# Two-layer decoder trunk on one core: order of the score matmuls, the affine steps, a weight-row sum and the last head's output-weight rows

## The chip, the core and the metric

The kernel runs on one core of a Trainium2 chip. A core has five engines that run in parallel, each with its own instruction queue, served in order: TensorE (PE, matmuls; its weight loads are listed as PEld), VectorE (DVE), ScalarE (ACT), GpSimd (POOL) and SyncE (SP, which only issues transfers). Transfers between the chip's memory and the core's SRAM go through 16 DMA engines; SP, ACT and POOL issue them into queues of their own. Matmuls write into eight PSUM banks of 128 partitions by 512 float32.

The metric is the device time of one execution in microseconds (us). The clock granted to TensorE was 0.997 of full speed in the profiled execution.

## The reference

A decoder trunk of two layers over 512 positions of width 1024 in float32, batch 1. Layer 0 mixes tokens with a causal pooling over windows, layer 1 with causal differential attention; a SwiGLU FFN of inner width 2816 follows each. Four layer norms in all.

```python
def _diff_attention(x, w_qkv, w_o, lam_p, subln_g, rel_table, lambda_init):
    qkv = x @ w_qkv
    # 8 heads, each with two score maps of width 64 and one value of width 128
    lam = exp(sum(lp[0]*lp[1])) - exp(sum(lp[2]*lp[3])) + lambda_init
    for qb in range(S // 128):
        s = einsum('bhcqd,bhckd->bhcqk', q_block, k[..., :kend]) * 64**-0.5
        s = where(rel >= 0, s + bias, -inf)
        p = softmax(s)
        a = p[:, :, 0] - lam * p[:, :, 1]
        outs.append(einsum('bhqk,bhkv->bhqv', a, v[:, :, :kend]))
    o = concatenate(outs)
    o = o * rsqrt(mean(o**2) + eps) * subln_g * (1 - lambda_init)
    return o @ w_o

def _swiglu(x, w_gate, w_up, w_down):
    return (silu(x @ w_gate) * (x @ w_up)) @ w_down

for i in range(2):
    h = pool(x) if i == 0 else diff_attention(x)
    x = layernorm(ALPHA * x + h)
    x = layernorm(ALPHA * x + swiglu(x))
```

## The kernel before, in words

**Numbers.** Every float32 matmul is made of three products of reduced-precision (float32r) operands: a value is split into a high part (a cast on ScalarE, line 123) and a low part (a subtraction on VectorE, line 124), and high x high, low x high, high x low are added in PSUM (`mm3`, lines 148 to 151). `split` does this; `ready(n)` (from line 126) splits weight rows up to number n, and `fetch` (line 107) loads the raw rows five ahead of that on SP's queue. Two of the raw rows, 74 and 75 of the weight array, are the sum of two rows each: a plain load on SP and then an accumulating transfer on POOL (line 113).

**Seven products in place of eight.** Most of the large matmuls are cut in 2x2 blocks and computed as seven products of sums of blocks, named P1, Q5, P6, Q3, P7, P2, Q4 in the order in which they run (`DOWN`). The second half of an FFN (the loop around line 936) runs these seven over six pairs of rows: 42 items, `d_0` to `d_41`; P2 is items 30 to 35, Q4 items 36 to 41. `prepare(j + 5, j + 4)` stands ahead of item j's matmuls (`multiply`, line 928): it issues the transfers and the splits of items some places ahead. Row sums are held in `r` (loads on SP, lines 541 and 544) and split into `d_..h` and `d_..l`; the left side is split into `xs`. Q4's last three items are done one half at a time, with the layer norm's pieces between (its reciprocal root is on POOL, line 199).

**The weight-row sums of the attention's values.** The values of all heads are computed in the same way: `values(p, ...)` (line 1076) for P1, P2, P6, P7, Q4, Q5, Q3, two weight pairs each. P6 uses `vt0`, `vt1`, the split of `tall`; P7 uses `vs0`, `vs1`, the split of `short` (part of the tile `vals`); Q4 uses `vu0`, `vu1`, the split of `tall` with one more row pair added. `tall` is the sum of three row pairs of 1 MB each: a load on SP and two accumulating transfers on POOL, all issued by `tall_step`, which the loop calls at the start of each product and which acts at Q3, P2 and Q4. The third accumulate into `tall` (line 1296) is issued after `vt0` and `vt1` have been split. `short` is a load on SP (line 1016) and an accumulate on POOL (line 1017). The tile of `tall` shares its buffer with the gains and offsets of the layer norms (`load_gb`), one buffer for both.

**The attention's heads.** The loop over heads (around line 1333) runs, in one pass h: the last part of head h-1's combination; the split of head h-1's values (`vh`, `vl`); in passes 1 to 4 one `affine` (lines 225 to 228), which multiplies and adds the previous norm's gain and offset on one 128-row block of the residual, two VectorE operations; queries and keys of head h and their splits, with `ready` between for rows that are needed later; head h-1's transposes (line 1183); scores of head h for the four blocks of 128 query rows (line 1142), softmax (VectorE line 1153, ScalarE line 1158), head h-1's product with the values (`mix`); and combinations of the two maps (VectorE lines 1167 to 1172). A pair of score banks is filled by three rounds of two matmuls, one on each half of the 128 rows of the array, one for each map. `root` and `scaled` are the norm of a head's output: `root(h-2)` and `scaled(h-2)` (tile `rso`) run two passes later.

In the last pass, h = 7, `ready` also splits rows of the output weight: `w92` and `w93` ahead of the query, `w94` and `w95` ahead of `scaled(5)` and of the split of the key. After the loop the output matmuls run (`wo`), one 128-row block s at a time, on rows `w92` to `w95`, with the norm of head 6, the transposes and the product of head 7 between them.

**What sets the order.** Each engine works its queue in the order in which the program names its instructions; waits between engines are put in by the framework from the tiles that are read and written. PSUM banks are handed out in turn, eight in all.

Of the kernel before, what the change touches and what calls it, by code (L numbers as in the profile page):

```python
# [16 lines left out]
ALU = mybir.AluOpType  # L17
# [7 lines left out]
SB = S // P  # L25
# [29 lines left out]
def trunk(ctx, tc, x, wall, pscale, lam_p, subln, table, lng, lnb, band, first, onehot, out):  # L55
    nc = tc.nc
# [145 lines left out]
    def norm(n, s, done=None):  # L202
        if (n, s) not in scales:
            spread_of(n, s)
        mv, rs = scales.pop((n, s))
        z = res[:, s, :]
        if not done:
            nc.vector.tensor_scalar(
                z, z, scalar1=mv[:, 0:1], scalar2=rs, op0=ALU.subtract, op1=ALU.mult
            )  # L210
            return
        gb = gbs[n]
        halves = [slice(d * 512, (d + 1) * 512) for d in range(2)]
        for c in halves:
            nc.vector.scalar_tensor_tensor(
                z[:, c], z[:, c], mv[:, 0:1], gb[:, 0, c], op0=ALU.subtract, op1=ALU.mult
            )
        for c in halves:
            nc.vector.scalar_tensor_tensor(
                z[:, c], z[:, c], rs, gb[:, 1, c], op0=ALU.mult, op1=ALU.add  # L220
            )
            done(s, c)

    def affine(n, s):
        z = res[:, s, :]
        gb = gbs[n]
        nc.vector.tensor_tensor(z, z, gb[:, 0, :], op=ALU.mult)
        nc.vector.tensor_tensor(z, z, gb[:, 1, :], op=ALU.add)
# [36 lines left out]
    def two_rows(c):  # L265
        return wall[vrow[c] : vrow[c] + 2].rearrange("r p t -> p r t")

    talls = []

    def tall_step(p):  # L270
        if p == "Q3":
            talls.append(keep.tile([P, 2, D], F32, tag="gb", name="tall"))
            nc.sync.dma_start(out=talls[0], in_=two_rows(0))
        elif p in ("P2", "Q4"):
            nc.gpsimd.dma_start(
                out=talls[0], in_=two_rows(1 if p == "P2" else 2), accum_op=ALU.add
            )

    lines = dram.tile([HEADS, LINE], F32, name="lines")

# [223 lines left out]
    def ffn(layer, late):  # L504
        n = 2 * layer + 1
        final = n == 2 * DEPTH - 1
# [3 lines left out]
        with tc.tile_pool(name=f"ffn{layer}", bufs=1) as fp:  # L510
# [58 lines left out]
            for k in range(HALF):  # L569
                j0 = index[k] = len(chunks)  # L570
                c = c0 + 4 * k
# [16 lines left out]
            for kind, j in steps:  # L588
                c, pair = chunks[j]
# [347 lines left out]
            done = store if final else None  # L937
            for p in DOWN:
                j0 = DOWN.index(p) * len(PAIRS)
                if not final:  # L940
                    tall_step(p)
                if p in ("P1", "Q5", "P2"):
                    banks[p] = [bank(f"{p}_{layer}_{s}") for s in range(2)]
                accs = banks[{"P1": "P1", "Q5": "Q5", "Q3": "Q5", "P2": "P2"}.get(p, "P1")]
                together = len(PAIRS) - (tail if p == "Q4" else 0)
                for i in range(together):
                    j = j0 + i
                    prepare(j + 5, j + 4)
                    if p == "Q4":
                        if i == together - 1:  # L950
                            prepare(len(items), len(items))
                            ready(c1 + FB + 2)
                        for s in range(2):
                            if i == s:
                                spread_of(n, s)
                            if i == s + 1:
                                norm(n, s)
                    multiply(j, accs, range(2))
                for s in range(2):
                    if p == "P1":  # L960
                        add_to(s, 0, accs[s], ALPHA)
                    elif p == "Q5":
                        add_to(2 + s, 1, accs[s], ALPHA)
                    elif p == "P6":
                        add_to(s, 1, accs[s], ALPHA, op=ALU.subtract)
                    elif p == "Q3":
                        add_to(s, 1, accs[s])
                        stat(n, s, 1)
                    elif p == "P7":
                        add_to(2 + s, 1, accs[s], op=ALU.subtract)  # L970
                        stat(n, 2 + s, 1)
                    elif p == "P2":
                        add_to(s, 0, accs[s])
                        stat(n, s, 0)
                    elif p == "Q4":
                        if s == 0 and not final:
                            turn(n, 0)
                        for i in range(len(PAIRS) - tail, len(PAIRS)):
                            if final and s == 0:
                                prepare(j0 + i + 5, j0 + i + 5)  # L980
                                if i == 1:
                                    spread_of(n, 0)
                                    spread_of(n, 1)
                                if i == 2:
                                    norm(n, 0, done)
                            multiply(j0 + i, accs, (s,))
                        add_to(2 + s, 0, accs[s], ALPHA)
                        stat(n, 2 + s, 0)
                        spread_of(n, 2 + s)
                        if final and s == 0:  # L990
                            norm(n, 1, done)
                        norm(n, 2 + s, done)
                        if not final:
                            if s == 0:
                                turn(n, 1)
                            ready(c1 + FB + 3 + s)
            base[0] = c1 + FB


    def attention():  # L1000
        n = 2
        with tc.tile_pool(name="attn", bufs=1) as ap:
            lp = ap.tile([P, 4, HD], F32, tag="bias", name="lp", bufs=2)
            nc.sync.dma_start(
                out=lp.rearrange("p a b -> p (a b)"),
# [52 lines left out]
            where = [base[0]]  # L1058
# [75 lines left out]
            def scores(h, q):  # L1134
                (qh, ql), (kh, kl) = qk[h, "q"], qk[h, "k"]
                wide = max((q + 1) * P, 256)
                accs = [bank(f"s{h}_{q}_{c}") for c in range(2)]
                qs = slice(q * P, (q + 1) * P)
                for i, (a, b) in enumerate(((qh, kh), (ql, kh), (qh, kl))):
                    for c in range(2):  # L1140
                        r = slice(c * HD, (c + 1) * HD)
                        nc.tensor.matmul(  # L1142
                            accs[c][:, :wide], a[r, qs], b[r, :wide], start=i == 0, stop=i == 2
                        )
                maps[h, q] = accs
# [186 lines left out]
            last = HEADS - 1  # L1332
            for h in range(HEADS):
                if h > 0:
                    combine(h - 1, 3)
                if h > 0:
                    split_values(h - 1)
                if h == 0:
                    scalars()
                if 0 < h <= SB:  # L1340
                    affine(n - 1, h - 1)
                if h == SB + 1:
                    load_gb(n)
                if h + 1 < HEADS:
                    load_bias(h + 1)
                if h > 0:
                    accs = [bank(f"{nm}{h}") for nm in "qk"]
                    w = take(2)
                    ready(where[0] + {1: 3, last: 2}.get(h, 1))
                    query(accs[0], w[0])  # L1350
                    split_query(h, "q", accs[0])
                    if h > 1:
                        root(h - 2)
                    query(accs[1], w[1])
                    ready(where[0] + (4 if h in (1, last) else 2))
                    if h > 1:
                        scaled(h - 2)
                    split_query(h, "k", accs[1])
                    if h == 1:
                        w = take(2)  # L1360
                        for r in range(2):
                            values("Q3", r, vc, w[r])
                        for s in range(2):
                            combined(part(0, 1, s), vc[s], part(0, 1, s), ALU.subtract)
                    transposed(h - 1)
                start_scores(h)
                for q in range(2):
                    scores(h, q)
                    softmax(h, q)
                if h == 0:  # L1370
                    for s in range(2):
                        combined(part(1, 1, s), vc[s], part(1, 1, s), ALU.subtract)
                for q in (2, 3):
                    scores(h, q)
                if h > 0:
                    mix(h - 1)
                for q in (2, 3):
                    combine(h, q - 2)
                    softmax(h, q)
                combine(h, 2)  # L1380
# [144 lines left out]
```

## Time and profile before

| | |
|---|---|
| median of 3 runs | 948.29 us (948.05 to 949.07) |
| the profiled execution's own time | 948.47 us |
| its span in the profile | 946.7 us |
| TensorE's granted clock | 0.997 |
| TensorE busy | 931.2 us, 5712 matmuls |
| VectorE, ScalarE, GpSimd busy | 787.3, 513.8, 126.5 us |
| moved by DMA | 211 MB, mean 223 GB/s |

The profile lists instructions as: start (us), duration (us), engine, line, operation, output <- inputs, partitions x elements, count; in square brackets how long the engine stood before it and what released it. A matmul's listed duration overlaps the next one's start, since matmuls are pipelined; consecutive starts show the rate. A DMA's row on its issuing engine is only the issue; landing times stand in the views by tile and by queue. In the view of waits, a row is engine, line, what it waited for, total us, times, longest. In the chain of waits a row is start, length and what held the last-ending work up.

### The profile page before, as it was taken

To read this page: it belongs to the slowest core of one execution; us is meant where nothing else is said; L and a number is where in the kernel's file an instruction comes from. 1 tells how busy PE (TensorE), PEld (TensorE's weight loads), DVE (VectorE), ACT (ScalarE), POOL (GpSimd) and SP (SyncE) were. 2 spreads that over 40 slices of the span, in tenths; PEclk is the share of its full clock that TensorE was granted. 3 is DMA by queue.
4 is the path that set the end of the run, shared out by engine and by line. 5 is a ranking of instruction groups with operands and counts; after the bars stand their busy time and mean duration, and the time that the engine had idled before them with its cause. 6 is when DMAs were issued, how large, how long until landed. Compare 5 with 4: busy or idle time off the path is not lost.

```text
span 946.7 us, 14942 instructions
## 1 busy us (share of the span) xinstructions
PE 931.2 (98%) x5712; PEld 829.9 (88%) x5712; DVE 787.3 (83%) x1158; ACT 513.8 (54%) x819; POOL 126.5 (13%) x152
## 2 busy tenths in 40 slices
PE   9999999999999999999999999999999999999996
PEld 8898899999988878887888878998899999988884
DVE  8858989999988489968887886789779999987778
ACT  6752344555564357666878753843345554664450
POOL 4120211110001201101111100211111110001101
PEclk9999999999999999999999999999999999999998
DMA  8386988986868996875666522396988886878952
GB/s 240 125 267 225 327 265 273 269 251 215 256 209 270 350 314 189 211 196 150 155 160 138 141 90 81 118 325 214 270 252 248 251 278 202 258 248 276 349 169 90
DMA packets 86038, 211.11 MB, mean 223 GB/s; under 512 B 15140, under 2 KB 26660, under 8 KB 85966
## 3 DMA queue, kind: packets, MB, share of 16 engines
q1 hardware_dynamic: 43420, 117.16, 37.5%
q0 software_dynamic: 18768, 58.20, 24.8%
q10 hardware_dynamic: 23778, 34.78, 10.2%
q8 instruction: 45, 0.74, 0.3%
q14 instruction: 27, 0.22, 0.1%
HBM read 173.40 MB, written 36.72 MB: 222 GB/s over the span
## 4 chain that ended last, share of the span: by engine, by line
PE 82%; DVE 9%; ACT 3%; DMA 3%; issue 2%; POOL 0%; DVEq 0%; ACTq 0%; POOLq 0%
PE A L861 17%; PE P L928 9%; PE C L861 9%; PE B L861 4%; PE Q L928 3%; PE g L151 3%; PE u L149 3%; PE u L150 3%; PE u L151 3%; PE g L149 3%; PE g L150 3%; PE va L1076 2%; PE s L1142 2%; DMA r<-tsum 1%; DMA r<-in_wall 1%
## 5 line engine op out<-in xcount | busy, mean ns | idle before, releaser
L607 DVE TENSOR_TENSOR raw<-raw,raw 128x1024 f32<-128x1024 f32 x56 | 68.3, 1219 | 0.5
L123 ACT CAST xs<-hid 128x512 fp32r<-128x512 f32 (+1 forms) x60 | 34.7, 582 | 24.4 <-DVE hid L775 24.4
L124 DVE TENSOR_TENSOR xs<-hid,xs 128x512 fp32r<-128x512 f32 (+1 forms) x60 | 38.5, 643 | 7.8 <-ACT xs L123 7.8
L1158 ACT ACTIVATE p<-p,mn 128x128 f32<-128x128 f32 (+3 forms) x64 | 35.2, 552 | 12.4 <-DVE mn L1153 12.4
L249 ACT ACTIVATE y<-pt,bT,gT 128x128 f32<-128x128 f32 x80 | 30.1, 456 | 19.4 <-PE pt L235 19.4
L706 POOL DMA_DIRECT2D b<-in_wall x20 | 14.0, 706 | 170.8 <-DMA tsum<-b 70.4
L767 POOL DMA_DIRECT2D xs<-ssum x24 | 17.4, 726 | 141.6 <-PE Q L928 68.5
L199 POOL TENSOR_TENSOR rs<-rs,mhalf 128x1 f32<-128x1 f32 x16 | 12.5, 784 | 152.0 <-DVE rs L198 112.6
L639 DVE TENSOR_TENSOR hid<-sg,u 128x512 f32<-128x512 f32 x16 | 11.0, 687 | 26.1 <-PE u L151 14.1
L743 ACT CAST v<-u 128x512 fp32r<-128x512 f32 x22 | 13.6, 620 | 27.7 <-DVE u L741 27.7
L706 POOL DMA_DIRECT2D hid<-in_wall x24 | 18.7, 823 | 74.4 <-DMA tsum<-hid 43.9
L1153 DVE CUSTOM_DVE_ANT_0 p<-s,bias 128x128 f32<-128x128 f32 (+3 forms) x64 | 28.0, 485 | 0.7 <-PE s L1142 0.7
L124 DVE TENSOR_TENSOR xt<-y,xt 128x512 fp32r<-128x512 f32 x20 | 13.6, 690 | 12.1 <-ACT xt L123 12.1
L190 DVE BATCH_NORM_STATS2 st<-res 128x6 f32<-128x512 f32 x32 | 22.2, 695 | 1.1
L887 ACT ACTIVATE sg<-sg 128x512 f32<-128x512 f32 x14 | 8.9, 633 | 25.7 <-DVE sg L880 25.7
L707 POOL DMA_DIRECT2D hid<-in_wall x12 | 14.8, 1233 | 58.5 <-DMA hid<-in_wall 51.1
L655 ACT CAST xs<-hid 128x1024 fp32r<-128x1024 f32 x8 | 8.4, 1051 | 26.0 <-DVE hid L672 11.6
L1142 PE MATMUL s<-heads 64*128 64x256 f32 (+2 forms) x168 | 20.0, 353 | 1.1 <-ACT heads L123 0.8
L1142 PEld LDWEIGHTS s<-heads 64*128 64x128 f32 x168 | 14.1, 185 | 5.2 <-issue 1.0
L1172 DVE SCALAR_TENSOR_TENSOR p<-p,sm,p 128x128 f32<-128x128 f32 (+3 forms) x32 | 17.7, 552 | 1.1
L876 DVE TENSOR_TENSOR hid<-C,hid 128x512 f32<-128x512 f32 x14 | 9.7, 691 | 10.4 <-PE C L861 8.8
L872 ACT COPY hid<-C 128x512 f32<-128x512 f32 x14 | 8.2, 589 | 18.5 <-PE C L861 18.5
(1187 smaller groups left out, 3666.3 us busy)
## 6 DMA issues: line engine op xcount, KB each, us to landing
raw<-in_wall SPq DMA_DIRECT2D x122, 512.0 KB, 4.8
r<-tsum SPq DMA_DIRECT2D x40, 512.0 KB, 4.5
hid<-in_wall POOLq DMA_DIRECT2D x36, 512.0 KB, 7.4
b<-in_wall POOLq DMA_DIRECT2D x30, 512.0 KB, 6.0
r<-in_wall SPq DMA_DIRECT2D x30, 512.0 KB, 4.6
tsum<-hid ACTq DMA_DIRECT2D x24, 512.0 KB, 5.6
ssum<-v ACTq DMA_DIRECT2D x22, 512.0 KB, 4.3
tsum<-b ACTq DMA_DIRECT2D x20, 512.0 KB, 4.9
```

Of the source, the lines that this page charges most:

```text
L123: nc.scalar.copy(dst_h, src)
L124: (low or nc.vector).tensor_tensor(dst_l, src, dst_h.bitcast(F32), op=ALU.subtract)
L149: nc.tensor.matmul(acc, ah, bh, start=start, stop=False)
L150: nc.tensor.matmul(acc, ah, bl, start=False, stop=False)
L151: nc.tensor.matmul(acc, al, bh, start=False, stop=stop)
L249: nc.scalar.activation(y[:, k, :], pt[:, k * P : (k + 1) * P], AF.Identity, bias=bT[:, n, kk : kk + 1], scale=gT[:, n, kk : kk + 1],)
L607: tt(t, raws[pair[0]], raws[pair[1]], op=ALU.add)
L706: nc.gpsimd.dma_start(out=t[:, j], in_=src[:, j])
L861: nc.tensor.matmul(o, w[:, c], x[:, kk, :], start=p in ("P1", "Q5", "P2") and f + kk + e == 0, stop=p in ("Q4", "Q3", "P2") and (f, kk, e) ...
L928: nc.tensor.matmul(accs[s], x[:, k, r], y[:, c], start=first and k == 0 and e == 0, stop=last and k == m - 1 and e == 2, skip_group_check= ...
L1142: nc.tensor.matmul(accs[c][:, :wide], a[r, qs], b[r, :wide], start=i == 0, stop=i == 2)
L1158: nc.scalar.activation(p, p, AF.Exp, bias=mn[:, q, c : c + 1], scale=-1.0, accum_out=sm[:, q, c : c + 1],)
```

## The change

Four things move; no matmul is added or removed.

- In `scores`, each round queues the second map's matmul ahead of the first map's.
- `tall_step` is called by step number: the load of `tall` at the start of P2 (it was Q3's start), the first accumulate at the third item of Q4 (it was P2's start), the second after the whole loop (it was Q4's start), so behind the `ready` calls of Q4's end that issue the accumulates of rows 74 and 75. The attention's set-up follows directly, with the load and the accumulate of `short`.
- The `affine` steps run in passes 2 to 5 in place of 1 to 4, and the next gains and offsets are loaded in pass 6 in place of 5.
- In pass 7 `ready` takes three output rows (`w92` to `w94`) ahead of the query, none ahead of the split of the key, and `w95` after head 6's product with the values, ahead of the first combination of head 7.

```diff
-    def tall_step(p):
-        if p == "Q3":
+    def tall_step(step):
+        if step == 0:
             talls.append(keep.tile([P, 2, D], F32, tag="gb", name="tall"))
             nc.sync.dma_start(out=talls[0], in_=two_rows(0))
-        elif p in ("P2", "Q4"):
-            nc.gpsimd.dma_start(
-                out=talls[0], in_=two_rows(1 if p == "P2" else 2), accum_op=ALU.add
-            )
+        else:
+            nc.gpsimd.dma_start(out=talls[0], in_=two_rows(step), accum_op=ALU.add)
...
             for p in DOWN:
                 j0 = DOWN.index(p) * len(PAIRS)
-                if not final:
-                    tall_step(p)
+                if p == "P2" and not final:
+                    tall_step(0)
...
+                    if (p, i) == ("Q4", 2) and not final:
+                        tall_step(1)
                     multiply(j, accs, range(2))
...
                             ready(c1 + FB + 3 + s)
+            if not final:
+                tall_step(2)
             base[0] = c1 + FB
...
                 for i, (a, b) in enumerate(((qh, kh), (ql, kh), (qh, kl))):
-                    for c in range(2):
+                    for c in (1, 0):
...
-                if 0 < h <= SB:
-                    affine(n - 1, h - 1)
-                if h == SB + 1:
+                if 1 < h <= SB + 1:
+                    affine(n - 1, h - 2)
+                if h == SB + 2:
                     load_gb(n)
...
-                    ready(where[0] + {1: 3, last: 2}.get(h, 1))
+                    ready(where[0] + {1: 3, last: 3}.get(h, 1))
...
-                    ready(where[0] + (4 if h in (1, last) else 2))
+                    ready(where[0] + {1: 4, last: 3}.get(h, 2))
...
                 if h > 0:
                     mix(h - 1)
+                if h == last:
+                    ready(where[0] + 4)
                 for q in (2, 3):
                     combine(h, q - 2)
                     softmax(h, q)
```

## The prediction

> **What bounds the kernel now.** I read the page first, then TensorE's waits, then the chain of waits, then timelines around each wait that the change touches. The page's first section:
>
> ```profile
> PE 931.2 (98%) x5712; PEld 829.9 (88%) x5712; DVE 787.3 (83%) x1158; ACT 513.8 (54%) x819; POOL 126.5 (13%) x152
> ```
>
> TensorE is busy 98% of the span. No matmul is removed, so the time moves only where the matmul stream stands still. The view of TensorE's waits lists those places (engine, line, releaser: total us, times, longest):
>
> ```profile
> PE P L928 <- DVE xs L124: 0.6, 1, 0.6
> ...
> PE vc L1076 <- DVE w78l L124: 0.5, 1, 0.5
> ```
>
> Each is one stall. A wait counts from the modelled end of the previous matmul, so what a stall costs is better read from start to start, against the 0.23 us at which 512-wide matmuls follow each other undisturbed. Everything else (VectorE 83%, DMA) matters only through when it lets TensorE go on. The sum is made against the profiled execution, 948.47 us (span 946.7 and 1.8 around it); the median of the runs is 948.29, so 0.18 is taken off at the end. About 0.2% (1.9 us) is what this measurement can tell from no change.
>
> **Weight-row sums, the gain.** Row loads of the first FFN's last phases come late while the sums' three 1 MB transfers run. The chain of waits, and TensorE's timeline there:
>
> ```profile
> 328.93 11.06 DMA r<-in_wall
> ```
> ```profile
> 341.29 0.39 PE L928 MATMUL P<-d_29h,xs 128*128 128x512 f32 x1
> 341.71 0.50 PE L928 MATMUL P<-d_30h,xs 128*128 128x512 f32 x1
> 342.04 0.40 PE L928 MATMUL P<-d_30l,xs 128*128 128x512 f32 x1
> 343.05 0.73 PE L928 MATMUL P<-d_30h,xs 128*128 128x512 f32 x2 [0.61 <-DVE xs L124]
> ```
>
> The gaps are 0.42 and 1.01 between starts where 0.23 is usual: 0.19 + 0.78 = 0.97 us. (A smaller one, 0.33, 0.10 too long, is left out.) A row transfer took 11.06 us, in a stretch in which both accumulating transfers of `tall` are in flight:
>
> ```profile
> L275 POOL DMA_DIRECT2D tall<-in_wall x2: 1208/1218/1227, 324.4 to 337.7; - x2
> ```
>
> After the change none of the three is issued before P2. I take the whole 0.97 as won; bounds 0 (the row loads fill the DMA by themselves) and -0.97, as the stall cannot give more than itself.
>
> **Weight-row sums, the loss.** What is moved must still land in time. The second accumulate was issued at 337.7, and its first reader, ScalarE's cast `vt0h`, ran at 394.23: 56 us of cover. Now GpSimd issues it after the loop, behind the accumulate into the second added row (raw75). GpSimd's timeline and the landings, by tile (minimum, median, maximum) and by issue (KB, us to landing):
>
> ```profile
> 381.95 0.90 POOL L113 DMA_DIRECT2D raw<-in_wall  x1 [2.25 <-ACT xt L123]
> ...
> 386.69 1.21 POOL L1017 DMA_DIRECT2D vals<-in_wall  x1 [3.63 <-DMA vals<-in_wall]
> ```
> ```profile
> DMA to landing us min/median/max: 4.0/7.1/9.9
> ```
> ```profile
> vals<-in_wall POOLq DMA_DIRECT2D x1, 1024.0 KB, 10.9
> tall<-in_wall POOLq DMA_DIRECT2D x1, 1024.0 KB, 8.5
> ```
>
> raw75's accumulate lands at 381.95 + 9.9 = 391.85 (the maximum is its own, as the longest of this queue's row loads there). The next 1 MB accumulate of the same queue, into `vals`, was issued at 386.69 and landed at 386.69 + 10.9 = 397.59. So it came 5.74 us behind raw75, although issued 5.2 us ahead of raw75's landing: I read this as a queue served in order. The moved accumulate is issued at 382.85, ahead of `vals`, and takes that place: it lands at 391.85 + 5.74 = 397.6, `vals` at 403.3. Now the readers, ScalarE, VectorE and TensorE in turn:
>
> ```profile
> 394.23 1.06 ACT L123 CAST vt0h<-tall 128x1024 fp32r<-128x1024 f32 x1
> ...
> 397.60 1.05 ACT L123 CAST vs0h<-vals 128x1024 fp32r<-128x1024 f32 x1 [0.87 <-DMA vals<-in_wall]
> ```
> ```profile
> 397.59 1.28 DVE L1259 TENSOR_TENSOR vals<-va,vals 128x512 f32<-128x512 f32 x2
> ```
> ```profile
> 398.42 0.47 PE L1076 MATMUL va<-vt0h,heads 128*128 128x512 f32 x1
> ...
> 409.43 0.39 PE L1076 MATMUL va<-vu0h,xt 128*128 128x512 f32 x1
> ```
>
> `vt0h` starts at 397.6 instead of 394.23, 3.37 late. Behind it VectorE does `vt0l`, `vt1l`, then reads both `va` banks (397.59), which product P6 overwrites; the first of the two reads ended at 397.59 + 0.64 = 398.23, and P6 began at 398.42: 0.19 of slack. So P6 starts 3.37 - 0.19 = 3.2 us late. ScalarE's `vt1h` and the query's square wait behind `vt0h`, but scores need those much later. `vals` at 403.3 instead of 397.6 delays `vs0h` by 5.7 against 3.2 that TensorE is late already; `vs0` is used 5.6 us after P6's start (24 matmuls of 0.23), at 407.2, and its cast and subtract (1.05 + 1.22) end at 405.6: covered. The third accumulate (issued when `vt1l` is read, about 401.2) lands 8.5 later at 409.7; `vu0`'s cast and subtract end at 412.0, and TensorE comes to it at 409.43 + 3.2 = 412.6: just covered. Bounds: 0, if the moved accumulate lands by 394.4; and with 8.5 us behind raw75 (the `tall` row) in place of 5.74, +5.9. I take +3.2, as the `vals` row is the same size, queue and moment.
>
> One rule of the Trainium skill speaks the other way: the page "DMA: Bandwidth & Descriptors", section "Bandwidth", has 6.15 us for 1 MB issued from GpSimd. Counted from issue that would land the transfer at about 389, before anybody reads it, and the sum would lose the 3.2. The trace has 8.5 and 10.9 for such transfers when they accumulate, so I let the rows decide.
>
> **Affine steps.** Head 1, the second of the two affine operations and what follows it on VectorE, and TensorE:
>
> ```profile
> 431.98 1.22 DVE L228 TENSOR_TENSOR res<-res,gb 128x1024 f32<-128x1024 f32 x1
> 433.12 1.22 DVE L124 TENSOR_TENSOR w78l<-raw,w78h 128x1024 fp32r<-128x1024 f32 x1
> ```
> ```profile
> 433.54 0.39 PE L1076 MATMUL vc<-w78h,heads 128*128 128x512 f32 x1
> 434.39 0.50 PE L1076 MATMUL vc<-w78l,heads 128*128 128x512 f32 x1 [0.46 <-DVE w78l L124]
> ```
>
> The gap is 0.85 - 0.23 = 0.62. Without the two (1.22 each) `w78l` can start up to 2.4 us sooner and the wait is gone: -0.62, bounds -0.62 and 0. The operations come back in head 5, where VectorE has room:
>
> ```profile
> 492.00:510.00 18.00, 18.00 (x103) 14.82 (x102) 12.81 (x36) 14.46 (x32) 3.01 (x3) 1.00 0.80 192
> ```
>
> The columns are window, length, then TensorE, its weight loads, VectorE, ScalarE, GpSimd. VectorE is busy for 12.81 of 18 there, so 2.4 more hides under a TensorE that is full; uncovered it would cost up to its 2.4. Gain and beta of the next norm are loaded one head later, far ahead of their use after head 7: 0.
>
> **Three rows ahead of head 7.** `w95l` leaves the place before the key split (VectorE, TensorE):
>
> ```profile
> 543.26 1.22 DVE L124 TENSOR_TENSOR w95l<-raw,w95h 128x1024 fp32r<-128x1024 f32 x1
> ...
> 546.44 0.68 DVE L124 TENSOR_TENSOR heads<-k,heads 128x512 fp32r<-128x512 f32 x1
> ...
> 549.80 0.17 DVE L1167 RECIPROCAL sm<-sm 128x2 f32<-128x2 f32 x1
> ...
> 556.58 0.75 DVE L1172 SCALAR_TENSOR_TENSOR p<-p,sm,p 128x512 f32<-128x512 f32 x1
> ```
> ```profile
> 547.18 2.49 PE L1142 MATMUL s<-heads 64*128 64x256 f32 x20 [0.34 <-DVE heads L124]
> ...
> 561.67 1.25 PE L1183 MATMUL at<-ident,p 128*128 128x128 f32 x10
> ```
>
> Everything behind it on VectorE moves up by its 1.2, and the scores wait for the key split: -1.2 in front of the scores. It comes back ahead of the combination at 549.80, and its cast stands on ScalarE behind the square of head 6's output:
>
> ```profile
> 552.52 0.62 ACT L123 CAST sqh<-sq 128x512 fp32r<-128x512 f32 x1
> ```
>
> On the clock moved up by 1.2, that ends at 551.9; `w95h`, a cast like `vt0h` (1.06), at 553.0; `w95l` at 554.2. VectorE was free for the combination at 548.6, so it stands for `w95h` and then works off a chain that ran from 549.80 to 557.33, 7.5 us: it ends at about 561.7. The transposes that read its last product come at 561.67 - 1.2 = 560.5, those of the last quarter some 0.3 later. So TensorE waits about 0.9 there, and head 6's norm, which VectorE does behind this chain, may cost some tenths more: the 1.2 is given back. I take 0; bounds -1.2 (the stand is made up) and +1.2 (the norm's lateness costs as much again).
>
> **Score order.** VectorE's softmax waits for scores, over all 64 halves, in total:
>
> ```profile
> L1153 DVE CUSTOM_DVE_ANT_0 p<-s,bias 128x128 f32<-128x128 f32 (+3 forms) x64 | 28.0, 485 | 0.7 <-PE s L1142 0.7
> ```
>
> That is VectorE's wait, 0.7 in all, and not TensorE's: same matmuls, other order. 0, bounds -0.3 and +0.3 (the last 0.34 wait of the row above).
>
> **The sum.** -0.97 + 3.2 - 0.62 + 0 + 0 = +1.6: 950.1 in a profiled execution, 949.9 as a median.
>
> **The rivals.** (A) The moved accumulate lands in time: for it, VectorE and ScalarE read at 394.23, 11.4 us after the issue at 382.85, and such a transfer has taken 8.5; against it, raw75 holds the queue to 391.85. Then -0.97 - 0.62 = -1.6: 946.7. (B) As A, and head 7 keeps its 1.2: for it, the chain is 7.5 long in the 11.9 between 549.80 and 561.67, so a shorter stand would be hidden; against it, `w95h` stands behind the square. Then 948.29 - 2.8 = 945.5, faster. (C) On the slow side, the queue takes 8.5 for 1 MB behind raw75, as in the `tall` row: landing at 400.35, P6 late by 5.9, 948.29 + 5.9 - 1.6 = 952.6; midway to the forecast 951.3. It makes the change slower by itself from a landing at 397.9 on, where 3.5 - 1.6 = 1.9. Against it, `vals` took 5.74. (D) The early stall does not go but moves: `tall`'s load now rides ahead of the last row loads on SP's queue in P2, so the 0.97 is lost again there: 950.9. For it, a row load took 11.06 beside an accumulate; against it, one plain load stands there in place of two accumulates.
>
> **How the numbers follow.** Forecast 0.45, with its own range 949.0 to 950.9; A 0.13, B 0.12, C 0.16, D 0.14. Slower by over 0.2% begins at 950.2, inside the forecast's own range: a third of it (0.14), C, and two thirds of D (0.09): 0.39. Faster begins at 946.4: B and 0.04 of A: 0.16. The rest, 0.45, is within. The range 946.0 to 951.9 leaves out the better half and more of B and half of C.
>
> **What would show it.** Right: no wait of TensorE at P L928 nor at vc in head 1, and a new one of about 3 us at P6, with ScalarE's `vt0h` waiting for a DMA of `tall` that lands near 397. In head 7 a short wait of the scores and a new one at the transposes, VectorE idle until `w95h`. Wrong: `vt0h` not waiting (then A or B), P L928 still waiting (D), VectorE not standing in head 7, or any wait in head 5.

## The result, and the profile after

| | before | after |
|---|---|---|
| median of 6 runs | 948.17 us (947.55 to 949.90) | 953.89 us (952.26 to 955.35) |
| ratio to before | | 1.0055, 95% interval 1.0042 to 1.0069 |
| the profiled execution, its span | 948.47, 946.7 | 954.01, 952.2 |
| TensorE's granted clock over the span | 0.997 | 0.993 |

The change makes the kernel about 5.2 us slower by the ratio (4.0 to 6.5), above the range on record (946.0 to 951.9). The same matmul can be found in both traces, as none is added or removed and each has its place in TensorE's order. The difference of its start times, read at a few places, is a ledger of what each place won or lost:

```
place (before's time)                        start before   after    shift
first FFN, layer 0        P<-d_28l           339.02         339.79   +0.77
behind the early stall    P<-d_30l           345.00         344.55   -0.44
last ahead of P6          k<-w73l            398.18         397.76   -0.42
P6's first                va<-vt0h           398.42         402.29   +3.86
P7's second               va<-vs0l           404.21         410.34   +6.12
head 1, ahead of its wait k<-w77l            433.31         439.44   +6.12
head 1, behind it         vc<-w78h           436.12         441.48   +5.36
head 7, ahead of scores   at<-p              544.44         549.86   +5.41
head 7, scores            s<-heads           548.37         552.51   +4.14
ahead of the transposes   wo<-w94h           561.43         565.57   +4.14
behind head 6's norm      wo<-w94h           565.96         571.42   +5.46
end                       P<-d_41h           937.30         942.74   +5.43
```

The +0.77 is there from the first matmuls on, where nothing is changed: it is the two executions' own difference (other executions shown below begin between -0.3 and +0.6). After it come -1.21, then +4.28 and +2.26 at P6, -0.76, -1.27 and +1.32.

TensorE's waits after the change, in the same view as before (engine, line, releaser: total us, times, longest):

```profile
PE va L1078 <- DVE vals L1261: 4.1, 1, 4.1
...
PE wo L149 <- DVE rso L1225: 0.6, 1, 0.6
...
PE at L1185 <- DVE p L1174: 0.2, 1, 0.2
```

The waits for the late rows, for head 1's `w78l` and for head 7's keys have left the list. Three are new: P6 for a PSUM bank, and two in head 7. A time in which an engine waits, as TensorE does here for P6, is called a stand below. The timeline of TensorE at P6:

```profile
397.76 0.39 PE L151 MATMUL k<-xt,w73l 128*128 128x512 f32 x1
402.29 0.77 PE L1078 MATMUL va<-vt0h,heads 128*128 128x512 f32 x1 [4.13 <-DVE vals L1261]
402.85 0.63 PE L1078 MATMUL va<-vt0l,heads 128*128 128x512 f32 x1
403.28 1.05 PE L1078 MATMUL va<-vt0h,heads 128*128 128x512 f32 x2
...
407.12 0.43 PE L1078 MATMUL va<-vt0h,heads 128*128 128x512 f32 x1
407.38 0.40 PE L1078 MATMUL va<-vt1h,heads 128*128 128x512 f32 x1
407.62 0.39 PE L1078 MATMUL va<-vt1l,heads 128*128 128x512 f32 x1
```

The gap is 4.53 from start to start, 4.3 more than usual. Then there is something that no row of before shows: from 402.29 to 407.12 the matmuls follow each other at 0.43 us instead of 0.23, though nothing is waited for. The same stretch by windows (window, length, TensorE, weight loads, VectorE, ScalarE, GpSimd, then TensorE's granted clock, DMA share, GB/s):

```profile
400.00:404.00 4.00, 1.71 (x4) 1.46 (x5) 3.33 (x5) 0.58 (x2) 1.18 (x1) 0.54 1.01 194
404.00:408.00 4.00, 4.00 (x12) 3.10 (x12) 2.69 (x3) 2.48 (x3) 0.00 (x0) 0.60 0.96 164
408.00:412.00 4.00, 4.00 (x20) 3.30 (x19) 1.53 (x3) 2.28 (x4) 0.00 (x0) 1.00 0.42 82
```

The granted clock is near one half in this stretch. From 404 to 408 TensorE counts as busy all the time and does 12 matmuls instead of 20. In the column of busy time this loss can't be seen; in the clock and in the count it can. Now what held P6 up. GpSimd, then ScalarE, then the landings of the transfers of `tall` (minimum, median, maximum):

```profile
364.48 1.23 POOL L275 DMA_DIRECT2D tall<-in_wall  x1
...
381.22 0.88 POOL L113 DMA_DIRECT2D raw<-in_wall  x1 [1.88 <-DMA lp<-in_lam]
381.81 1.54 POOL L275 DMA_DIRECT2D tall<-in_wall  x1
...
391.54 1.19 POOL L1019 DMA_DIRECT2D vals<-in_wall  x1 [7.97 <-DMA vals<-in_wall]
```
```profile
398.10 1.04 ACT L123 CAST vt0h<-tall 128x1024 fp32r<-128x1024 f32 x1 [4.11 <-DMA tall<-in_wall]
...
404.23 1.05 ACT L123 CAST vs0h<-vals 128x1024 fp32r<-128x1024 f32 x1 [3.65 <-DMA vals<-in_wall]
```
```profile
DMA to landing us min/median/max: 8.4/12.8/16.3
```

The second accumulate, issued at 381.81 behind raw row 75's, took the 16.3 us and landed at 398.1; raw row 75's had landed at 391.0, 7.1 us before it. The chain behind it is the predicted one: `vt0h`, `vt0l`, `vt1l`, VectorE's reads of the `va` banks, P6.

In head 7, VectorE stood for `w95h` as forecast:

```profile
558.25 1.47 DVE L124 TENSOR_TENSOR w95l<-raw,w95h 128x1024 fp32r<-128x1024 f32 x1 [4.35 <-ACT w95h L123]
```

### The profile page after: what moved, and what is told of

Read it like the earlier page. It is cut to its first block, busy times and chain, and to the rows that moved or that the text cites. A ratio compares the mean times of both kernels' runs of the same rounds, so it can differ in the third digit from the quotient of the medians.

```text
span 952.2 us, 14942 instructions
## 1 busy us (share of the span) xinstructions
PE 933.8 (98%) x5712; PEld 832.4 (87%) x5712; DVE 788.1 (83%) x1158; ACT 514.4 (54%) x819; POOL 126.5 (13%) x152
## 4 chain that ended last, share of the span: by engine, by line
PE 89%; DVE 5%; DMA 2%; ACT 2%; issue 1%; POOL 0%; DVEq 0%; SPq 0%; POOLq 0%; ACTq 0%
PE A L859 17%; PE P L926 14%; PE C L859 8%; PE Q L926 6%; PE B L859 4%; PE g L151 3%; PE u L151 3%; PE u L149 3%; PE u L150 3%; PE g L149 3%; PE g L150 3%; PE s L1144 2%; PE va L1078 2%; DMA tall<-in_wall 2%; PE q L149 1%; PE q L151 1%
## 5 line engine op out<-in xcount | busy, mean ns | idle before, releaser
L249 ACT ACTIVATE y<-pt,bT,gT 128x128 f32<-128x128 f32 x80 | 30.0, 455 | 19.4 <-PE pt L235 19.4
L199 POOL TENSOR_TENSOR rs<-rs,mhalf 128x1 f32<-128x1 f32 x16 | 12.6, 792 | 163.0 <-DVE rs L198 123.6
L705 POOL DMA_DIRECT2D hid<-in_wall x12 | 14.8, 1233 | 56.3 <-DMA hid<-in_wall 49.6
L653 ACT CAST xs<-hid 128x1024 fp32r<-128x1024 f32 x8 | 8.4, 1051 | 23.8 <-DVE hid L670 11.6
L124 POOL TENSOR_TENSOR sql<-sq,sqh 128x512 fp32r<-128x512 f32 x7 | 9.0, 1293 | 65.0 <-ACT sqh L123 65.0
```

The lines of the kernel that those rows point to most:

```text
L124: (low or nc.vector).tensor_tensor(dst_l, src, dst_h.bitcast(F32), op=ALU.subtract)
L249: nc.scalar.activation(y[:, k, :], pt[:, k * P : (k + 1) * P], AF.Identity, bias=bT[:, n, kk : kk + 1], scale=gT[:, n, kk : kk + 1],)
```

## The experiments

Each is compared with runs of the kernel before on the same chip (its median there in brackets).

**The weight-row sum alone.** The kernel before with the three `tall_step` edits only.

```diff
-                if not final:
-                    tall_step(p)
+                if p == "P2" and not final:
+                    tall_step(0)
...
+                    if (p, i) == ("Q4", 2) and not final:
+                        tall_step(1)
...
+            if not final:
+                tall_step(2)
```

> Only the weight-row sum is moved; scores, affine steps and head 7 as before. My theory (the loss is all in this part: product P6 waits for the second accumulate, and then runs at a lower clock for about 5 us): the early stall of 1.2 us goes, P6 loses about 6.6, so about +5.4 on before, near 953.6, and TensorE's clock is again near 0.55 right after the stall. Rival (the loss comes from the four parts together, DMA or SRAM traffic spread over the attention): well under +4.

Median 954.40 (947.95), ratio 1.0072, interval 1.0055 to 1.0089. The whole loss is in this part; the intervals overlap, so that it is more than the loss of the whole change can't be told. Its profiled execution has the early stall gone (1.22 won at the ledger's places), TensorE at a stand of 4.1 us at P6, and 3.4 us of slow matmuls behind it. It is the fastest of the four: its granted clock is 0.996 over the span, and the other three, at 0.993 to 0.995, took 954.2 to 955.4 us.

**All but the weight-row sum.** The changed kernel with `tall_step` as before.

```diff
-                if p == "P2" and not final:
-                    tall_step(0)
+                if not final:
+                    tall_step(p)
...
-                    if (p, i) == ("Q4", 2) and not final:
-                        tall_step(1)
...
-            if not final:
-                tall_step(2)
```

> The change without the weight-row sum: score order, affine steps and head 7 as in the changed kernel. My theory: head 1 gains 0.6 to 0.8, head 7 gains 1.3 at the scores and gives 1.3 back at its transposes, score order nothing: 947.3 to 947.6, no wait at P6, clock 0.997. Rival (as above): above 949.

Median 947.67 (947.95), ratio 0.9997, interval 0.9988 to 1.0006: no change that can be told. The ledger of its trace has -0.76 in head 1, -1.28 at head 7's scores and +1.32 at its transposes and norm: head 7 gives back what it wins, and some 0.7 us of head 1 should remain. The interval, from 1.1 us less to 0.6 us more, neither shows nor excludes it.

**Score order alone.**

```diff
-                    for c in range(2):
+                    for c in (1, 0):
```

> Only the order of the two score matmuls of each round is changed. My theory: nothing, within 0.1% of before. Rival (the pair frees the second map earlier and VectorE's softmax saves time on the path): 0.3 to 2 us less; or (the pair now waits for the later bank first) 0.3 to 2 us more.

Median 948.20 (947.88), ratio 1.0001, interval 0.9993 to 1.0010: nothing, as forecast. VectorE's wait for scores is 0.7 us in all, before and after.

**Is the slow clock set off by the stand? Idle matmuls in the wait.** Idle matmuls are ones whose result nobody reads. In the changed kernel, ahead of P6:

```diff
+            for i in range(18):
+                nc.tensor.matmul(
+                    vb[1], xt[:, 0, 0, 0, :P],
+                    xt[:, 0, 0, 0:2, :].rearrange("p k t -> p (k t)"), start=True, stop=True,
+                )
             for r in range(2):
                 values("P6", r, va, wide6[r])
```

> The changed kernel with 18 idle matmuls (512 wide, into a score-free bank, results not used) queued on TensorE ahead of product P6, 18 x 0.227 = 4.1 us, so that TensorE does not stand while it waits. If the slow clock after the stall is set off by TensorE's standing, P6 begins at the same time but runs at 0.23 us a matmul: 2.3 us less than the changed kernel, near 951.5. If the lower clock has another cause (a supply limit, contention for SRAM with the transfers), nothing is won: near 953.9.

Median 951.09 (947.95), ratio 1.0037, interval 1.0024 to 1.0050. TensorE's timeline:

```profile
397.23 4.24 PE L1305 MATMUL vb<-xt 128*128 128x512 f32 x18
401.77 0.47 PE L1078 MATMUL va<-vt0h,heads 128*128 128x512 f32 x1 [0.30 <-DVE vals L1261]
402.08 0.39 PE L1078 MATMUL va<-vt0l,heads 128*128 128x512 f32 x1
```

P6 begins as late as before the filling, and runs at 0.23 us a matmul from its second on. The excess over before falls from 5.7 to 3.1 us by medians; 2.6 of it, against 2.26 in the ledger, was the slow clock. The transfers were running as in the changed kernel (the second accumulate took 16.4 us), so they are not its cause.

**How short a stand does no harm? 9 and 13 idle matmuls.**

```diff
-            for i in range(18):
+            for i in range(9):
```
```diff
-            for i in range(18):
+            for i in range(13):
```

> The changed kernel with 9 idle matmuls ahead of P6 instead of 18: TensorE stands about 2.2 us instead of 4.3. If a stand must fill a whole window of about 3.4 us to lower the clock, the clock stays up and the time is fill18's, near 951.1. If any stand lowers it for some time, near 952 to 953.9.

> The changed kernel with 13 idle matmuls (3.0 us) ahead of P6: TensorE stands 1.3 to 2.2 us there. Theory (a stand of about 3 us or more lowers the clock, a shorter one does not): the clock stays up, near fill18's 951.1. Rival (any stand of over a microsecond lowers it): near 952.7 as with 9.

With 9, median 952.71 (947.88), ratio 1.0049, interval 1.0036 to 1.0063; with 13, 951.85 (948.74), ratio 1.0043, interval 1.0027 to 1.0060. The two profiled executions, first 9:

```profile
397.24 2.20 PE L1305 MATMUL vb<-xt 128*128 128x512 f32 x9
402.43 0.77 PE L1078 MATMUL va<-vt0h,heads 128*128 128x512 f32 x1 [2.99 <-DVE vals L1261]
402.99 0.63 PE L1078 MATMUL va<-vt0l,heads 128*128 128x512 f32 x1
```

then 13:

```profile
397.31 3.11 PE L1305 MATMUL vb<-xt 128*128 128x512 f32 x13
401.12 0.47 PE L1078 MATMUL va<-vt0h,heads 128*128 128x512 f32 x1 [0.70 <-DVE vals L1261]
401.43 0.39 PE L1078 MATMUL va<-vt0l,heads 128*128 128x512 f32 x1
```

The expected 2.2 us with 9 was wrong, since the transfer landed later in that execution (17.2 us after its issue): the stand was 3.0 to 3.2 us, and the granted clock was one half for 3.4 us. At a stand of 0.7 to 0.9, with 13, it did not fall. In the traces of this document it falls at every stand of 3.1 us or more, counted from start to start, and at none of 1 us or less; lengths between were not tried. The landing moves from run to run, which blurs both medians, but each run's granted clock over the span tells the runs apart (3.4 us at one half take some 0.002 off it). With 9, three runs at 0.995 took 952.3 to 953.9 us and one at 0.998 took 950.9; with 13, three at 0.997 or 0.998 took 951.4 to 952.1 and one at 0.995 took 954.1; the five with 18 were all at 0.997 or 0.998. The Trainium skill, page "TensorE: Matmul & The Clock Gate", section "HAM oscillation — how this bites in real kernels", gives the rule: no idle gaps of TensorE above about 3.4 us, or the clock goes to one half. The trace agrees with the half (0.43 against 0.23 us); a stand of 3.0 to 3.2 us was enough here, and the measurement decides.

**One place earlier in the queue.** The second accumulate ahead of the accumulates of rows 74 and 75.

```diff
+                            if s == 0:
+                                tall_step(2)
                             ready(c1 + FB + 3 + s)
-            if not final:
-                tall_step(2)
```

> The changed kernel with the second accumulate issued one place earlier, ahead of the accumulates of raw rows 74 and 75 (its issue waits for the first to land, about 377). If the place in GpSimd's queue is the cause, it lands by about 388, P6 does not wait and the clock does not fall: 6.6 us less than the changed kernel, near 947. If it is the amount of traffic in that stretch, whatever the order, P6 still waits some us or the wait moves to the products after it: 950 or more.

Median 953.02 (947.95), ratio 1.0053, interval 1.0038 to 1.0069: nearly nothing is won. The expected cause, the place in GpSimd's queue, was only half of it. P6 now begins on time, and the next product stands instead. TensorE, then ScalarE, then the plain load of `vals` (landing):

```profile
403.08 0.39 PE L1078 MATMUL va<-vt1h,heads 128*128 128x512 f32 x1
407.94 0.80 PE L1078 MATMUL va<-vs0h,heads 128*128 128x512 f32 x1 [4.47 <-ACT vals L1308]
408.54 0.63 PE L1078 MATMUL va<-vs0l,heads 128*128 128x512 f32 x1
```
```profile
404.93 1.04 ACT L123 CAST vs0h<-vals 128x1024 fp32r<-128x1024 f32 x1 [8.87 <-DMA vals<-in_wall]
```
```profile
DMA to landing us min/median/max: 17.9/17.9/17.9
```

The load of `vals` on SP's queue, a plain 1 MB that took 12.6 us in the changed kernel and 7.2 before, takes 17.9 here; its accumulate follows at 396.58 and lands 8.3 later, at 404.9. ScalarE stands for it with `vs0h`, and behind `vs0h` on its queue are the copies that empty the `va` banks, which P7's matmuls need. So TensorE stands for 4.6, and the clock falls again. In both runs the wait goes to whichever 1 MB transfer comes last in this stretch. (The fastest of the four runs, 951.5 us, has a granted clock of 0.998 over the span, so its clock did not fall.)

**The first accumulate early, the second as in the change.**

```diff
+                if p == "Q4" and not final:
+                    tall_step(1)
...
-                    if (p, i) == ("Q4", 2) and not final:
-                        tall_step(1)
```

> The changed kernel with the first accumulate at Q4's start, and the second still after the loop, behind raw row 75's. Theory (the second accumulate's own late issue makes P6 wait; the first is harmless where the change has it): P6 still waits 3.5 to 4.5 us and the clock falls: 952 to 954. Rival (the first accumulate, issued at 364, pushes all transfers behind it late): the second lands 3 us or more earlier and the time is below 950.

Median 950.99 (948.74), ratio 1.0023, interval 1.0013 to 1.0033: between the two theories. Issue rows and landings of `tall`:

```profile
L275 POOL DMA_DIRECT2D tall<-in_wall x2: 1227/1388/1550, 344.7 to 381.2; - x2
...
DMA to landing us min/median/max: 8.4/12.9/14.8
```

The second accumulate takes 14.8 us instead of 16.3. TensorE stands for 3.1 us instead of 4.3, and 1.4 us after P6's start it still falls to half speed, for 3.4 us (stand and slow matmuls cost 4.65 by the ledger, against 6.54). So the first accumulate, at Q4's third item, was not harmless: with it out of the way the second lands sooner. One way in which it does harm can be followed on GpSimd, by the accumulate of raw row 74, first in the changed kernel, then here:

```profile
377.84 0.91 POOL L113 DMA_DIRECT2D raw<-in_wall  x1 [4.39 <-ACT rp L249]
```
```profile
372.86 0.90 POOL L113 DMA_DIRECT2D raw<-in_wall  x1 [0.24 <-issue]
```

It needs the plain load of that row. Beside the first accumulate this load takes 10.7 us and lands at 377.12; here it takes 4.4 (4.8 before). The first row names ScalarE's L249 as what ended the wait, but that only came last by the profile: here the accumulate is issued 2.7 us before that line first runs. So in the changed kernel row 74's accumulate lands at 386.81 instead of 378.42, in the stretch in which row 75's, the second accumulate and the load of `vals` are under way.

**Both accumulates early.**

```diff
+                if p == "Q4" and not final:
+                    tall_step(1)
+                    tall_step(2)
```

> The changed kernel with both accumulates into the weight-row sum issued at Q4's start, one behind the other (load at P2's start as in the change). My theory now (the stretch from 376 to 405 has more transfers than the DMA engines can carry in time, whatever their order, while 355 to 375 has room): both land before 375, P6 and P7 do not wait, the clock stays; the early stall is still gone. No_tall's 947.7 less 1.1: 946.6. Rival (the two accumulates now delay the last row loads of the FFN, or the norm's roots behind them on GpSimd): a stall at P L926 or at the transposes, 947.7 or more.

Median 946.28 (947.88), ratio 0.9980, interval 0.9972 to 0.9989: as expected within 0.3 us. The issues, and the first reader on ScalarE:

```profile
L275 POOL DMA_DIRECT2D tall<-in_wall x2: 1208/1218/1227, 346.4 to 358.6; - x2
```
```profile
392.76 1.06 ACT L123 CAST vt0h<-tall 128x1024 fp32r<-128x1024 f32 x1
```

With issues at 346.4 and 358.6 and 12 us each, the sum is in place by 371. `vt0h` waits for nothing, and the early stall is gone all the same (-1.21).

**And w95 ahead of head 6's product.** As the last, with

```diff
+                if h == last:
+                    ready(where[0] + 4)
                 if h > 0:
                     mix(h - 1)
-                if h == last:
-                    ready(where[0] + 4)
```

> As both_q4, and w95 split ahead of head 6's product with the values in place of behind it, so that its cast runs while ScalarE waits for that product. If VectorE's stand for that cast is what gave back head 7's gain, the wait at head 7's transposes and at the norm goes: 1.3 less than both_q4, near 945.3. If the give-back is the norm of head 6 or VectorE's work itself, nothing changes.

Median 945.35 (947.88), ratio 0.9970, interval 0.9959 to 0.9980: faster than both kernels. In the ledger of its trace, head 7's scores win 1.24 and the +1.32 behind them is gone. By medians the step is 0.9. VectorE's stand:

```profile
548.92 1.23 DVE L124 TENSOR_TENSOR w95l<-raw,w95h 128x1024 fp32r<-128x1024 f32 x1 [1.97 <-ACT w95h L123]
```

It is 1.97 instead of 4.35 us, which the rest of the pass hides.

## Why the prediction was wrong, point by point

**The early stall: right.** The whole of it went, 1.21 where 0.97 was forecast (two smaller gaps beside it, 0.10 and 0.11, went with it). Rival D, that it only moves, did not happen.

**P6's wait: the mechanism right, its size half.** This is the term that was mis-sized: +3.2 on record, +6.5 measured, 4.28 of stand and 2.26 of slow matmuls behind it. Two steps of the working failed.

First, the landing. It was put at 397.6, 5.74 us behind raw row 75's, by taking everything ahead of the second accumulate to be where before had it. Row 75's lands at 391.0 instead of 391.85, as it is issued 0.7 us sooner; but the second accumulate, issued 1.0 us sooner than assumed, comes 7.1 us behind it, 16.3 from its issue in place of 14.75, and lands at 398.1. TensorE stands ready for P6 0.4 us sooner than before, and the slack of 0.19 was none (P6 follows `vt0h` by 4.19 us in both traces). These three turn the 3.2 into 4.3. What was left out is the first accumulate, whose new place was priced at nothing: with it out of the way (its experiment above) the second takes 14.8 us from its issue and the stand is 3.1, as in the working. That the 14.8 is met to the tenth is partly luck, as two differences cancel: from its issue it is 8.7 us to row 75's landing and 6.1 more to its own, where 9.0 and 5.74 were taken. And it is one execution, though in the five profiled executions with the changed order (the changed kernel, the weight-row sum alone and the three with idle matmuls) the second accumulate took 15.7 to 17.2.

Second, and larger, "So P6 starts 3.37 - 0.19 = 3.2 us late" was taken as the whole cost: the working counted a stand of TensorE at its length. It costs more: behind stands of 3.1 to 4.6 us, TensorE worked 3.2 to 5.5 us at half its clock. Filling the wait with idle matmuls shows that the stand sets this off. Neither the sum nor rival C had it, and it made a slowdown of about 3 us one of nearly 6.

**The queue served in order: not the whole cause.** The working read the landing as a place in GpSimd's queue. Putting the transfer one place earlier made another 1 MB transfer, on another queue, late by as much. What helped was to take both accumulates out of the stretch from 375 to 405: issued before 360, they leave no wait there. That the DMA engines are short of time in it, rather than something else that the transfers share, is argued and not shown: between 385 and 395 their busy share is 1.06 in the kernel before, in the changed one and with both accumulates early alike, and only between 395 and 405 does it differ (0.69, 1.02 and 0.64).

**Affine steps: right.** -0.76 by the ledger against -0.62 (the gap behind it, 0.11 too long, went too), and no wait in head 5. No median shows it by itself.

**Three rows ahead of head 7: right, but for how the give-back divides.** -1.27 at the scores against -1.2; +1.32 behind them against 0.9 and some tenths; net nothing. Of the 1.32 the transposes have 0.5, where 0.9 was forecast, and the matmuls behind head 6's norm 0.8, where some tenths were. The stand for `w95h`, 4.35 us, is what gives it back, as taking it away gives the gain.

**Score order: right.** Nothing.

The forecast's sum with the measured 6.5 in place of 3.2 is 948.29 - 0.97 - 0.62 + 6.5 = 953.2, in the interval of the measured time. The range's upper end, 951.9, was set by rival C, whose price knew only the length of the stand.

## What to carry to other kernels

A stand of the matmul engine of some three microseconds or more is not priced at its length: look at the granted clock behind it, and add what the next matmuls lose at half speed. A transfer that is moved out of one crowded stretch has to be followed to where it goes; there, sum the bytes between the moves and the first reader before asking about their order in one queue, and look for the stretch with room (here 345 to 371, where both accumulates then ran). And a split that is only moved behind a wait on another engine gives back what it won; put it ahead of that wait, so that its cast runs while the engine would stand.

## What the runs showed of the hardware that was not expected

- TensorE's rate fell to half (0.43 us for 512 columns in place of 0.23) at stands of 3.1 to 4.6 us and came back by itself. It stayed full at stands of 0.3 and 0.7 us.
- The stretches of half clock were of two lengths only: 3.41 us (the weight-row sum alone, 9 idle matmuls, the first accumulate early) and 6.83 us (the changed kernel, one place earlier). They do not begin with the stand: in the changed kernel the stretch runs from 400.35, 1.9 us before P6, to 407.17, and with the first accumulate early from 401.64, 1.4 us after P6 had begun. In each of the five traces it begins a whole number of steps of 3.413 us after the first entry in the record of the granted clock (in the changed kernel 7.81 and 400.35, 115 steps). So the price of a stand depends on where it falls, and not on its length alone. It is paid for the part of the stretch in which TensorE works: in the changed kernel 4.88 us at 0.43 in place of 0.23 make 2.3, with 2.26 in the ledger.
- The plain 1 MB load of `vals` on SP's queue took 5.9 to 8.5 us in the six traces in which the second accumulate is done or not yet issued for most of that time (7.2 before, 5.9 with the first accumulate early), and 11.6 to 17.9 in the six in which it runs beside it (12.6 in the changed kernel, 17.9 with the second accumulate one place earlier). A queue of its own did not keep it from being slowed, to well under half its rate at worst. Row 74's accumulate is late in the same six, and by which shared part the load is slowed was not tried.
